# 64-row and 64-column attention matmuls made 128x128 in a two-layer streaming encoder step

## The chip, the cores and the metric

One core of a Trainium2 chip runs the whole step. The metric is the device time of one execution in microseconds (us). The engines are called TensorE (PE in the profile, its weight loads PEld), VectorE (DVE), ScalarE (ACT), GpSimd (POOL) and SyncE (SP, which only issues the transfers here). TensorE multiplies a stationary operand (`lhsT`, up to 128 rows by 128 columns) with a moving one (`rhs`, up to 512 columns) and writes PSUM; each matmul is preceded by a weight load.

## The reference, cut to what matters

Two layers run over 592 tokens: 16 meta tokens, 512 new prompt tokens and 64 new sample tokens, which have 256 cached keys of their own. Each layer normalises its input, projects it with one wide weight, and sums three gated branches (attention, a gated linear recurrence, causal pooling). The attention branch is what the change touches:

```python
s_idx = relu(einsum('bthd,bsd->bths', qi, ki))        # indexer: 4 heads of 64, one key of 64
score = einsum('bth,bths->bts', wi, s_idx)            # chunk-causal mask, then top k of the keys
logits = einsum('bthd,btjhd->bthj', q, k_gathered) * 64 ** -0.5   # 8 heads of 64
p = softmax(where(valid, logits, -inf))
out = einsum('bthj,btjhd->bthd', p, v_gathered)
```

Prompt queries see the meta tokens and the prompt up to the end of their own 64-token chunk, and keep 128 keys; sample queries see their 256 cached and 64 new keys and keep 80. The output holds the final activations, the new keys and values, and the recurrent states.

## The kernel before, in words

All weights are split into two float32r parts, and a projection is three matmuls per 128 input channels, all at line 266 (`mm3`). `c_project` makes 128 output channels for 296 (layer 0) or mostly 288 (layer 1) tokens at a time: 24 matmuls into one PSUM tile `acc` of three. `t_project` makes 256 or 324 channels for up to 128 tokens.

Attention and recurrence are written as Python generators, `index(j)`, `attend(j)`, `lru(g)`; after each projection `spend` credits them with a share of its time and runs steps of them, so that their instructions are emitted in between. The tile framework then orders every engine's instructions by simulating the program with its own costs: an instruction that is ready early in that simulation can be moved far ahead on its engine. Each engine executes its list in order. Buffers are slots of pools, and an instruction waits for its slot: `sc`, `rel` and `pt` have one, `lpa` (the logits) has two, the PSUM tiles `pq` and `pT` two each, and `pv` (the attention output) one.

Queries and keys lie with two heads of 64 along the partitions: `QK[:, 0:4]` queries, `QK[:, 4:8]` keys, `QI[:, 0:2]` indexer queries, `QI[:, 2]` the indexer key in both halves. Values `V` lie with keys along the partitions. Query tiles 0 to 3 are the prompt in blocks of 128, tile 4 is the sample. Prompt tile j has 144, 272, 400 or 528 keys (j+1 blocks of 128 and 16 more; 528 is done as two spans of 264).

- `index(j)`: for each of the four heads a 64-row matmul (line 434; for the sample 64x64 ones, written twice for both halves of the output, lines 429 and 431), a relu on ScalarE, a weighted sum on VectorE into `sc`; then 16 (sample: 10) rounds of max and replace on VectorE, and a bias tile.
- `attend(j)`, `logits`: for a pair of heads a 64-row matmul for each head and span (line 504; sample 64x64, lines 497 and 500), a masked minimum on VectorE (line 508), exp on ScalarE (514), reciprocal on VectorE (516), scaling on GpSimd (517, and 519 for the last 16 keys into `prem`).
- `values(u)`: for one head the blocks of probabilities are transposed on TensorE (529), copied to `pt` by ScalarE or VectorE (533, 531), and multiplied with 64 columns of values into one 64-partition half of `pv` (540). `rest(a)` adds the last 16 keys of four heads together with two 128x128 matmuls (547 to 551).
- At the end of `attend` one ScalarE copy puts `pv` into `QK` (568), where the queries were.

Other float32 matmuls on the full array are those of the recurrence gates (line 638, `lru`) and of the pooling map (741). Rotary (`rope`, lines 354 to 357) takes VectorE, GpSimd twice and VectorE again for each 128 channels. Attention on the projections' order: sample and first two tiles are indexed during the key and query projections; `attend(4)`, `attend(0)`, `index(2)`, `attend(1)`, `index(3)`, `attend(2)`, `attend(3)` follow during the gates, the first two branches and the pooling, and everything left is emitted at `side.drain()` ahead of the attention's own gate.

Of the kernel before, what the change touches and what calls it, by code (L numbers as in the profile page):

```python
# [9 lines left out]
F32 = mybir.dt.float32  # L10
F32R = mybir.dt.float32r
BF16 = mybir.dt.bfloat16
AF = mybir.ActivationFunctionType
# [3 lines left out]
D = 1024  # L17
NM = 16
SEQ = 512
NP = NM + SEQ  # L20
NS = 64
NT = NP + NS
# [18 lines left out]
class Side:  # L41
    """Steps of work emitted in between the projections."""
# [25 lines left out]
def build(ctx, tc, ap):  # L68
# [30 lines left out]
    nc.gpsimd.memset(vrem, 0.0)  # L99
    hb = const.tile([128, L, 8], F32)  # L100
# [167 lines left out]
    def t_project(ch, cols, src, evac, tiles=TILES):  # L268
        """Token-major: evac(t, psum) for each tile of tokens."""
# [16 lines left out]
    def c_project(ch, nk, src, pieces, evac, w=None, off=0, stride=128):  # L286
        """Channel-major: evac(piece, c0, n, psum) for each piece of the tokens."""
# [19 lines left out]
    def layer(l, xn, x_src, last):  # L307
# [7 lines left out]
        QK = big.tile([128, 8, NT], F32, name="QK", tag="big")  # L315
        VI = big.tile([128, 5 * 512 + 3 * NT], F32, name="VI", tag="big")
        V = VI[:, :2560].rearrange("p (t c) -> p t c", t=5)
        QI = VI[:, 2560:].rearrange("p (t c) -> p t c", t=3)
# [4 lines left out]
        vs = CH[0:64, 2304:2816]  # L323
# [72 lines left out]
        def ev_v(half_i):  # L396
            def f(t, c0, rows, p):
# [3 lines left out]
                if t == 4:  # L401
                    nc.sync.dma_start(vs[:, a], V[16:80, 4, a])
            return f

# [10 lines left out]
        def index(j):  # L415
# [5 lines left out]
            spans = [(0, 320)] if sample else kspan(j)  # L421
            for h in range(4):
                o = 64 * (h % 2)
                q = QI[o:o + 64, h // 2, q0:q0 + (64 if sample else 128)]
                for a, n in spans:
                    p = psq.tile([128, 512], F32, name="pq", tag="qk")
                    if sample:
                        for z in (0, 64):
                            nc.tensor.matmul(p[z:z + 64, 0:256], lhsT=q, rhs=kx[o:o + 64, :], start=True, stop=True)
                        for z in (0, 64):  # L430
                            nc.tensor.matmul(p[z:z + 64, 256:320], lhsT=q, rhs=QI[o:o + 64, 2, NP:NT],
                                             start=True, stop=True)
                    else:
                        nc.tensor.matmul(p[:rows, :n], lhsT=q, rhs=QI[o:o + 64, 2, a:a + n], start=True, stop=True)  # L434
# [26 lines left out]
        def attend(j):  # L461
            """The sample's tile (4) has two heads of 64 queries along the partitions; the others one of 128."""
# [7 lines left out]
            blocks = [(0, 128), (1, 128), (2, 64)] if sample else [(i, 128) for i in range(j + 1)]  # L470
            pv = psv.tile([128, 4, 128], F32, name="pv", tag="pv")
            P = {}
            if not sample:
# [465 lines left out]
```

## Time and profile before

| | us |
|---|---|
| three runs | 1294.51, 1295.75, 1297.30 (median 1295.75) |
| span of the profiled execution, first to last instruction | 1294.3 |
| PE busy in the span | 1266.2 (98%) |
| DVE busy | 745.7 (58%) |
| ACT busy | 467.4 (36%) |
| POOL busy | 284.2 (22%) |

The page gives the profiled execution by its span alone; the median of the runs lies 1.45 us above that span. A matmul's busy time in the profile is its modelled way through the array, about 0.3 us, while the next one starts after 0.13 us; so the time that a matmul costs is read from the starts of its neighbours, not from its own duration. A float32 matmul is two MATMUL rows (two passes), a float32r matmul or a transpose is one. The forms are written rows*columns of the stationary operand, then the moving operand.

### The profile page before, as it was taken

The numbers are of one execution on the slowest core, as the hardware profiler recorded it, in microseconds if no ns is written. First come the engines' busy times: TensorE is split into PE (matmuls) and PEld (weight loads), VectorE is DVE, ScalarE is ACT, GpSimd is POOL, SyncE is SP. The second block draws the span as 40 slices with busy tenths as digits, with TensorE's granted clock in tenths as the row PEclk, the third lists the DMA queues.
The fourth block names the chain that finished last, engine by engine and source line by source line (L and its number), as shares of the span: only waits on it lengthen the run. The fifth ranks groups of instructions, "written<-read, shape, count | busy, mean of one in ns | idle before, by whom it ended". The sixth has DMA issues, their size and how long they took to land.

```text
span 1294.3 us, 22304 instructions
## 1 busy us (share of the span) xinstructions
PE 1266.2 (98%) x9060; PEld 1177.7 (91%) x9060; DVE 745.7 (58%) x1588; ACT 467.4 (36%) x921; POOL 284.2 (22%) x329
## 2 busy tenths in 40 slices
PE   5999989999999999999999999899999999999998
PEld 5999978898988899999999999789799888999997
DVE  6388993665954334434363889848396543344343
ACT  5344543332333322332343446432333332233232
POOL 5122432021123320011012234311111332101121
PEclk9999999999999999999999999999999999999999
DMA  9321221221222022221353212112122212222212
GB/s 288 112 71 65 104 83 50 65 66 57 67 93 66 33 90 82 82 82 67 105 165 127 66 65 104 59 56 75 50 74 90 76 33 75 81 86 78 94 55 74
DMA packets 38024, 107.16 MB, mean 83 GB/s; under 512 B 6912, under 2 KB 10048, under 8 KB 37664
## 3 DMA queue, kind: packets, MB, share of 16 engines
q1 hardware_dynamic: 37920, 105.72, 25.0%
q8 instruction: 71, 1.16, 0.4%
q14 instruction: 33, 0.27, 0.1%
HBM read 95.35 MB, written 10.09 MB: 81 GB/s over the span
## 4 chain that ended last, share of the span: by engine, by line
PE 87%; DVE 9%; POOL 1%; issue 1%; ACT 1%; DMA 1%; SPq 0%; POOLq 0%; DVEq 0%; ACTq 0%
PE acc L266 73%; PE pv L540 4%; PE pq L504 3%; PE pT L529 2%; DVE wl L190 2%; PE pq L434 1%; DVE rt L354 1%; DVE lxc L628 1%; DVE sc L451 1%; PE pv L551 1%; PE pg L741 1%; DVE lT L654 1%; DVE m L450 1%; DVE QK L357 1%; POOL QK L356 1%
## 5 line engine op out<-in xcount | busy, mean ns | idle before, releaser
L266 PE MATMUL acc<-xh,wh 128*128 128x296 f32 (+1 forms) x1728 | 524.0, 303 | 0.0
L266 PE MATMUL acc<-xh,wl 128*128 128x296 f32 (+1 forms) x1728 | 521.5, 302 | 0.0
L266 PE MATMUL acc<-xl,wh 128*128 128x296 f32 (+1 forms) x1728 | 520.4, 301 | 0.0
L266 PEld LDWEIGHTS acc<-xh,wh 128*128 128x128 f32 x1728 | 326.7, 189 | 12.2 <-issue 8.0
L266 PEld LDWEIGHTS acc<-xl,wh 128*128 128x128 f32 x1728 | 327.2, 189 | 7.8 <-issue 5.3
L190 DVE TENSOR_TENSOR wl<-wr,wh 128x1024 fp32r<-128x1024 f32 (+1 forms) x158 | 210.7, 1335 | 212.1 <-ACT wh L189 209.2
L266 PEld LDWEIGHTS acc<-xh,wl 128*128 128x128 f32 x1728 | 325.5, 188 | 7.9 <-issue 5.6
L189 ACT ACTIVATE wh<-wr 128x1024 fp32r<-128x1024 f32 (+1 forms) x158 | 166.2, 1054 | 277.3 <-PE acc L266 256.8
L517 POOL TENSOR_SCALAR lpa<-lpa,mn 128x128 f32<-128x128 f32 (+4 forms) x72 | 84.2, 1170 | 281.2 <-DVE mn L516 238.7
L266 PE MATMUL acc<-yh,wh 128*128 128x296 f32 (+1 forms) x384 | 115.9, 302 | 0.0
L266 PE MATMUL acc<-yl,wh 128*128 128x296 f32 (+1 forms) x384 | 115.3, 300 | 0.0
L266 PE MATMUL acc<-yh,wl 128*128 128x296 f32 (+1 forms) x384 | 114.6, 299 | 0.0
L266 PE MATMUL acc<-wh,ml 128*128 128x256 f32 (+2 forms) x320 | 89.4, 281 | 0.0
L266 PE MATMUL acc<-wh,mh 128*128 128x256 f32 (+2 forms) x320 | 88.5, 280 | 0.0
L266 PE MATMUL acc<-wl,mh 128*128 128x256 f32 (+2 forms) x320 | 88.5, 280 | 0.0
L450 DVE MAX8 m<-sc 64x8 f32<-64x144 f32 (+4 forms) x148 | 74.7, 504 | 4.0 <-POOL sc L445 1.0
L266 PEld LDWEIGHTS acc<-yh,wh 128*128 128x128 f32 x384 | 72.3, 188 | 5.1 <-issue 4.2
L266 PEld LDWEIGHTS acc<-yl,wh 128*128 128x128 f32 x384 | 72.3, 188 | 2.9 <-issue 2.9
L266 PEld LDWEIGHTS acc<-yh,wl 128*128 128x128 f32 x384 | 72.2, 188 | 1.4 <-issue 1.4
L451 DVE MATCH_REPLACE8 sc<-m,sc 64x144 f32<-64x144 f32 (+4 forms) x148 | 72.5, 490 | 0.1
L514 ACT ACTIVATE lpa<-lpa,mn 128x144 f32<-128x144 f32 (+4 forms) x72 | 41.2, 572 | 72.6 <-DVE mn L508 70.1
L699 ACT ACTIVATE e<-acc 128x296 f32<-128x296 f32 (+1 forms) x96 | 38.9, 405 | 71.4 <-PE acc L266 71.3
(194 smaller groups left out, 1688.2 us busy)
## 6 DMA issues: line engine op xcount, KB each, us to landing
wr<-wc SPq DMA_DIRECT2D x108, 512.0 KB, 3.3
wr<-wb SPq DMA_DIRECT2D x24, 512.0 KB, 3.3
wr<-wo SPq DMA_DIRECT2D x16, 512.0 KB, 3.7
kT<-QK SPq DMA_DIRECT2D x2, 1184.0 KB, 4.2
xi<-xin SPq DMA_DIRECT2D x8, 256.0 KB, 7.6
wr<-wv SPq DMA_DIRECT2D x4, 512.0 KB, 6.4
v_p<-VI SPq DMA_DIRECT2D x16, 128.0 KB, 1.9
xo<-xin SPq DMA_DIRECT2D x8, 256.0 KB, 2.6
```

Source lines behind the costliest of these rows:

```text
L189: nc.scalar.activation(h[:, :size], r[:, :size], AF.Copy)
L190: nc.vector.tensor_sub(lo[:, :size], r[:, :size], h[:, :size].bitcast(F32))
L266: nc.tensor.matmul(out, lhsT=a, rhs=b, start=(i == 0), stop=(i == n - 1))
L354: nc.vector.stream_shuffle(t[:r, c0:], x[:, c0:], SWAP)
L450: nc.vector.max(m8[rr], sc[rr, :w])
L451: nc.vector.match_replace(sc[rr, :w], m8[rr], sc[rr, :w], TAKEN)
L504: nc.tensor.matmul(p[:, :n], lhsT=QK[o:o + 64, u // 2, q0:q0 + 128], rhs=QK[o:o + 64, 4 + u // 2, a:a + n], start=True, stop=True)
L514: nc.scalar.activation(t[:, :w], t[:, :w], AF.Exp, bias=mn[:, i:i + 1], scale=-1.0, accum_out=mn[:, 2:3])
L517: nc.gpsimd.tensor_scalar(t[:, :wm], t[:, :wm], mn[:, 3:4], None, op0=ALU.mult)
L529: nc.tensor.transpose(ps[:n, i], t[:, 128 * i:128 * i + n], ident)
L540: nc.tensor.matmul(pv[o:o + 64, h // 2, :nq], lhsT=val(i, n, h), rhs=pt[:n, i, c:c + nq], start=(i == 0 and (sample or u < 2)), stop=(samp ...
L699: nc.scalar.activation(e[:, c0:c0 + nn], p, AF.Tanh, scale=0.5)
```

## The change

Every attention and indexer matmul gets a stationary operand of 128 rows and 128 columns.

Logits and indexer scores: the queries of one head are copied by GpSimd into a tile whose other 64 rows stay zero, and the matmul runs over both heads' keys. For the indexer that tile is `qiz` (four heads; two copies for a prompt tile, four for the sample, made before the first head). For the prompt logits it is `qz`, two buffers of two heads each, kept behind `QK` and `VI` in their slots; two copies for each pair of heads. For the sample `qzs` has head 2u in rows and columns 0 to 63 and head 2u+1 in the others; two copies in all. The zeros are written in `late_loads`, once for each layer.

Values: `values` takes both heads of a pair, transposes both, copies both to a `pt` of twice the size, and multiplies 128 columns of values with 256 columns of probabilities. Half of the product is not wanted, and only the wanted halves are copied out. `pv` is now a tile for each four heads (`[128, 2, 2, 128]`, still one slot), copied out by two ScalarE instructions in `rest(a)`; `rest` has four matmuls instead of two. The sample's third block of keys is padded with zero rows in `vs` and zero probabilities.

To make room, `bd` (recurrence weights) and `gB` (norm weights) share one slot, which they take in turn: norm 0, recurrence 0, norm 1, recurrence 1, final norm.

```diff
+    qiz = const.tile([128, 4, 128], F32)
+    nc.gpsimd.memset(qiz, 0.0)
...
-        g = lay.tile([128, D], F32, name="gB")
+        g = lay.tile([128, D], F32, name="gB", tag="gb")
...
+        QK_ = big.tile([128, 8 * NT + 256], F32, name="QK", tag="big")
+        VI = big.tile([128, VE + 768], F32, name="VI", tag="big")
+        qz = [QK_[:, 8 * NT:].rearrange("p (t c) -> p t c", t=2),
+              VI[:, VE:VE + 256].rearrange("p (t c) -> p t c", t=2)]
+        qzs = VI[:, VE + 256:].rearrange("p (t c) -> p t c", t=4)
-        vs = CH[0:64, 2304:2816]
+        vs = CH[:, 2304:2816]
-        bd = lay.tile([128, 2, 4, 128], F32, name="bd")
+        bd = lay.tile([128, 2, 4, 128], F32, name="bd", tag="gb")
...
+            nc.gpsimd.memset(qz[0], 0.0)
+            nc.gpsimd.memset(VI[:, VE:], 0.0)
+            nc.gpsimd.memset(vs[64:128], 0.0)
...
+            for par in range(2):
+                o = 64 * par
+                for z in range(0, 128, nq):
+                    nc.gpsimd.tensor_copy(qiz[o:o + 64, par::2, z:z + nq], QI[o:o + 64, 0:2, q0:q0 + nq])
             for h in range(4):
-                o = 64 * (h % 2)
-                q = QI[o:o + 64, h // 2, q0:q0 + (64 if sample else 128)]
+                q = qiz[:, h]
...
-                        for z in (0, 64):
-                            nc.tensor.matmul(p[z:z + 64, 0:256], lhsT=q, rhs=kx[o:o + 64, :], start=True, stop=True)
...
+                        nc.tensor.matmul(p[:, 0:256], lhsT=q, rhs=kx, start=True, stop=True)
+                        nc.tensor.matmul(p[:, 256:320], lhsT=q, rhs=QI[:, 2, NP:NT], start=True, stop=True)
-                        nc.tensor.matmul(p[:rows, :n], lhsT=q, rhs=QI[o:o + 64, 2, a:a + n], start=True, stop=True)
+                        nc.tensor.matmul(p[:, :n], lhsT=q, rhs=QI[:, 2, a:a + n], start=True, stop=True)
...
+            if sample:
+                for o in (0, 64):
+                    nc.gpsimd.tensor_copy(qzs[o:o + 64, :, o:o + 64], QK[o:o + 64, 0:4, NP:NT])
...
+                if not sample:
+                    i = units[0] // 2
+                    for o in (0, 64):
+                        nc.gpsimd.tensor_copy(qz[i % 2][o:o + 64, o // 64], QK[o:o + 64, i, q0:q0 + 128])
...
-                            nc.tensor.matmul(p[:, :n], lhsT=QK[o:o + 64, u // 2, q0:q0 + 128],
-                                             rhs=QK[o:o + 64, 4 + u // 2, a:a + n], start=True, stop=True)
+                            nc.tensor.matmul(p[:, :n], lhsT=qz[u // 2 % 2][:, u % 2], rhs=QK[:, 4 + u // 2, a:a + n],
+                                             start=True, stop=True)
...
+            def values(units):
+                i = units[0] if sample else units[0] // 2
+                pt = tmp.tile([128, 4, 2, 128], F32, name="pt", tag="pt")
+                for n, u in enumerate(units):
+                    t = P.pop(u)
+                    ps = psm.tile([128, 4, 128], F32, name="pT", tag="ms")
+                    for k in range(nb):
+                        nc.tensor.transpose(ps[:, k], t[:, 128 * k:128 * k + 128], ident)
+                    if u % 2:
+                        nc.vector.tensor_copy(pt[:, :nb, n], ps[:, :nb])
+                    else:
+                        nc.scalar.activation(pt[:, :nb, n], ps[:, :nb], AF.Copy)
...
+                if i % 2 == 0:
+                    pvs[i // 2] = psv.tile([128, 2, 2, 128], F32, name="pv", tag="pv")
+                for k in range(nb):
+                    nc.tensor.matmul(pvs[i // 2][:, i % 2], lhsT=val(k, i), rhs=pt[:, k],
+                                     start=(k == 0 and i % 2 == 0), stop=False, skip_group_check=True)
...
-                for i in (2 * a, 2 * a + 1):
-                    nc.tensor.matmul(pv[:, i], lhsT=vrem[:, i], rhs=pr, start=False, stop=True,
-                                     skip_group_check=True)
+                for i in range(2):
+                    for n in range(2):
+                        nc.tensor.matmul(pv[:, i, n], lhsT=vrem[:, 2 * a + i], rhs=pr, start=False, stop=True,
+                                         skip_group_check=True)
+                for n in range(2):
+                    o = 64 * n
+                    nc.scalar.activation(QK[o:o + 64, 2 * a:2 * a + 2, q0:q0 + 128], pv[o:o + 64, :, n], AF.Copy)
...
-            nc.scalar.activation(QK[:, 0:4, q0:q0 + nq], pv[:, :, :nq], AF.Copy)
```

## Rows read from the trace of the kernel before

**Rows 1.** Page, part 4: shares of the chain that ended last.
```profile
PE 87%; DVE 9%; POOL 1%; issue 1%; ACT 1%; DMA 1%; SPq 0%; POOLq 0%; DVEq 0%; ACTq 0%
```

**Rows 2.** TensorE's waits: us in total, times, longest.
```profile
PE pq L581 <- DVE QK L357: 4.1, 2, 3.6
PE pq L497 <- DVE mn L508: 2.7, 1, 2.7
```

**Rows 3.** Busy us by stretch: PE, PEld, DVE, ACT, POOL, then clock, DMA, GB/s.
```profile
110.00:190.00 80.00, 75.45 (x526) 70.09 (x524) 76.06 (x175) 42.92 (x68) 29.66 (x28) 0.98 0.27 89
324.00:360.00 36.00, 36.00 (x260) 35.53 (x259) 34.31 (x70) 11.31 (x21) 5.49 (x10) 1.00 0.23 74
```

**Rows 4.** Line 266 alone in the two attention stretches: length, busy us, matmuls.
```profile
190.00:478.00 288.00, 221.19 (x1456) 1.00 0.20 64
822.00:1098.00 276.00, 209.74 (x1418) 1.00 0.20 65
```

**Rows 5.** Chain of waits, projections of 296 and 288 tokens: start, us, what.
```profile
232.00 3.00 PE acc L266 x22
...
1059.33 3.20 PE acc L266 x24
```

**Rows 6.** TensorE timeline at 426 us: start, us, line, tiles, forms, count.
```profile
426.52 0.38 PE L266 MATMUL acc<-xl,wh 128*128 128x296 f32 x1
426.83 0.71 PE L504 MATMUL pq<-QK 64*128 64x264 f32 x2
427.47 0.40 PE L266 MATMUL acc<-xh,wl 128*128 128x296 f32 x1
427.81 1.09 PE L540 MATMUL pv<-pt,VI 128*64 128x128 f32 x8
428.82 0.40 PE L266 MATMUL acc<-xh,wh 128*128 128x296 f32 x1
429.07 0.30 PE L266 MATMUL acc<-xl,wh 128*128 128x296 f32 x1
```

**Rows 7.** TensorE timeline at 87 us, float32 on the full array.
```profile
87.10 0.30 PE L266 MATMUL acc<-xh,wl 128*128 128x296 f32 x1
87.23 1.17 PE L638 MATMUL pg<-lxc,bd 128*128 128x298 f32 x4
88.02 0.52 PE L266 MATMUL acc<-xh,wh 128*128 128x296 f32 x1
88.38 0.30 PE L266 MATMUL acc<-xl,wh 128*128 128x296 f32 x1
```

**Rows 8.** TensorE timeline at 366 us, two heads' logits in a row.
```profile
366.43 0.30 PE L266 MATMUL acc<-xh,wl 128*128 128x296 f32 x1
366.65 0.94 PE L504 MATMUL pq<-QK 64*128 64x400 f32 x4
367.53 0.40 PE L266 MATMUL acc<-xh,wh 128*128 128x296 f32 x1
367.77 0.30 PE L266 MATMUL acc<-xl,wh 128*128 128x296 f32 x1
```

**Rows 9.** GpSimd groups by form: a small copy, a scaling of 128 columns.
```profile
L517 POOL TENSOR_SCALAR lpa<-lpa,mn 128x128 f32<-128x128 f32 x16 | 11.0, 690 | 54.7 <-DVE mn L516 54.7
L382 POOL COPY wd<-wt 4x64 f32<-4x64 f32 x2 | 0.5, 228 | 0.0
```

**Rows 10.** Timelines of VectorE and GpSimd near 123 us.
```profile
122.78 2.00 POOL L356 TENSOR_TENSOR QK<-QK,rope_c 128x592 f32<-128x592 f32 x1
123.39 2.04 DVE L628 SCALAR_TENSOR_TENSOR lxc<-CH,prm,lxc 128x595 f32<-128x595 f32 x1
127.21 0.82 DVE L628 SCALAR_TENSOR_TENSOR lxc<-CH,prm,lxc 128x595 f32<-128x595 f32 x1
```

**Rows 11.** Line 266 alone, from the start of attention to the denser VectorE stretches.
```profile
190.00:324.00 134.00, 103.08 (x688) 1.00 0.18 58
822.00:940.00 118.00, 86.98 (x576) 1.00 0.17 58
```

More of the change, by code (lines that the diff above doesn't have):

```diff
@@ L469, in attend @@
             b = bias.pop(j)
[L470 to L473, printed above, removed]
+            nb = 3 if sample else j + 1
+            if sample:
+                for o in (0, 64):
+                    nc.gpsimd.tensor_copy(qzs[o:o + 64, :, o:o + 64], QK[o:o + 64, 0:4, NP:NT])
+            else:
                 for h in range(NH):
@@ L494, in logits @@
                         if sample:
-                            q = [QK[z:z + 64, u, NP:NT] for z in (0, 64)]
-                            for z in (0, 64):
-                                nc.tensor.matmul(p[z:z + 64, 0:256], lhsT=q[z // 64], rhs=kc[z:z + 64, u, :],
-                                                 start=True, stop=True)
-                            for z in (0, 64):
-                                nc.tensor.matmul(p[z:z + 64, 256:320], lhsT=q[z // 64],
-                                                 rhs=QK[z:z + 64, 4 + u, NP:NT], start=True, stop=True)
-                        else:
-                            o = 64 * (u % 2)
-                            nc.tensor.matmul(p[:, :n], lhsT=QK[o:o + 64, u // 2, q0:q0 + 128],
-                                             rhs=QK[o:o + 64, 4 + u // 2, a:a + n], start=True, stop=True)
+                            nc.tensor.matmul(p[:, 0:256], lhsT=qzs[:, u], rhs=kc[:, u, :], start=True, stop=True)
+                            nc.tensor.matmul(p[:, 256:320], lhsT=qzs[:, u], rhs=QK[:, 4 + u, NP:NT],
+                                             start=True, stop=True)
+                        else:
+                            nc.tensor.matmul(p[:, :n], lhsT=qz[u // 2 % 2][:, u % 2], rhs=QK[:, 4 + u // 2, a:a + n],
+                                             start=True, stop=True)
                     for u in units:
@@ L517, in logits @@
                     nc.gpsimd.tensor_scalar(t[:, :wm], t[:, :wm], mn[:, 3:4], None, op0=ALU.mult)
-                    if not sample:
+                    if sample:
+                        nc.gpsimd.memset(t[:, w:384], 0.0)
+                    else:
                         nc.gpsimd.tensor_scalar(prem[:, u // 4, u % 4, 0:16], t[:, wm:w], mn[:, 3:4], None,
@@ L521, in logits @@
                     P[u] = t
-            def values(u):
-                t = P.pop(u)
-                pt = tmp.tile([128, 4, 128], F32, name="pt", tag="pt")
-                ps = psm.tile([128, 4, 128], F32, name="pT", tag="ms")
-                nf = sum(1 for _, n in blocks if n == 128)
-                for i, n in blocks:
-                    nc.tensor.transpose(ps[:n, i], t[:, 128 * i:128 * i + n], ident)
-                if u % 2:
-                    nc.vector.tensor_copy(pt[:, :nf], ps[:, :nf])
-                else:
-                    nc.scalar.activation(pt[:, :nf], ps[:, :nf], AF.Copy)
-                if sample:
-                    nc.scalar.activation(pt[:64, 2], ps[:64, 2], AF.Copy)
-                for h in ((2 * u, 2 * u + 1) if sample else (u,)):
-                    o = 64 * (h % 2)
-                    c = o if sample else 0
-                    for i, n in blocks:
-                        nc.tensor.matmul(pv[o:o + 64, h // 2, :nq], lhsT=val(i, n, h), rhs=pt[:n, i, c:c + nq],
-                                         start=(i == 0 and (sample or u < 2)), stop=(sample and i == 2),
-                                         skip_group_check=not sample)
+            def values(units):
[8 more added lines that the diff above has]
+                        nc.vector.tensor_copy(pt[:, :nb, n], ps[:, :nb])
+                    else:
+                        nc.scalar.activation(pt[:, :nb, n], ps[:, :nb], AF.Copy)
+                if sample:
+                    if i == 0:
+                        pvs[0] = psv.tile([128, 4, 128], F32, name="pv", tag="pv")
+                    for k in range(nb):
+                        nc.tensor.matmul(pvs[0][:, i], lhsT=val(k, i), rhs=pt[:, k, 0], start=(k == 0),
+                                         stop=(k == nb - 1))
+                    return
+                if i % 2 == 0:
+                    pvs[i // 2] = psv.tile([128, 2, 2, 128], F32, name="pv", tag="pv")
+                for k in range(nb):
+                    nc.tensor.matmul(pvs[i // 2][:, i % 2], lhsT=val(k, i), rhs=pt[:, k],
+                                     start=(k == 0 and i % 2 == 0), stop=False, skip_group_check=True)
@@ L557, in attend @@
                     yield w * 2.5
-                    values(u)
+                    values([u])
+                for o in (0, 64):
+                    nc.scalar.activation(QK[o:o + 64, 0:4, NP:NT], pvs[0][o:o + 64, :, o:o + 64], AF.Copy)
             else:
@@ L562, in attend @@
                     yield w * 2.5
-                    values(2 * u)
-                    values(2 * u + 1)
+                    values([2 * u, 2 * u + 1])
                     if u % 2:
```

21 lines of the change are left out of this document (11 added, 10 removed).

## The prediction

> **What bounds the kernel now.** I read first the chain of waits: TensorE holds 87% of it and VectorE 9% [rows 1], so a microsecond taken from TensorE's list is a microsecond of the kernel wherever VectorE does not hold it up. TensorE's own waits then show where that is: apart from the start, the two long ones are 3.6 us for the last rotary of layer 0 and 2.7 us for the minimum of the sample's logits in layer 1 [rows 2]. Both end the stretch in which tiles 4, 0 and 1 are indexed beside the recurrence and the rotaries: there VectorE is busy 76.06 of 80 us [rows 3]. In the attention stretches behind it the projections alone make 1456 and 1418 matmuls [rows 4]. They follow each other every 3.00/22 = 0.136 us in layer 0 and 3.20/24 = 0.133 us in layer 1 [rows 5]. So 288.0 - 1456 x 0.1364 = 89.5 us and 276.0 - 1418 x 0.1333 = 86.9 us of these stretches are spent on other matmuls. That is where the change works.
>
> **Why small forms cost more than their columns.** The timeline at 87 us has float32 matmuls on the full array: from 87.10 to 88.38 us are two projections (0.27) and four passes of 298 columns, so a pass costs (1.28 - 0.27)/4 = 0.252 us, or 0.846 ns a column, with nothing at either end [rows 7]. At 426 us the array changes its form twice: from 426.52 to 429.07 us are three projections (0.41), two passes of 264 columns on 64 rows and eight passes of 128 columns to 64 columns [rows 6]. At 0.846 ns a column these passes are 0.45 + 0.87 = 1.31 us, and they take 2.14: two visits to a small form cost 0.83 us on top. About half of it is seen ahead of and behind each visit, where the next start is 0.31 to 0.34 us away instead of 0.136.
>
> The opposite effect is there too. Two heads of 64 rows, 400 columns each, issued in a row at 366 us, take 367.77 - 366.43 - 0.27 = 1.07 us for four passes [rows 8], where four on the full array would take 4 x 400 x 0.846 = 1.35: the heads run partly together, and padding loses that. It is in the measured stretches already. The Trainium skill ("TensorE: Matmul & The Clock Gate", Part 3: Packing small matmuls) makes this the rule and speaks against the change: matmuls in different row groups run concurrently, and a small one takes as long as a full one. By that rule, with every two heads together, the logits and scores of these stretches would lose some 2 us a layer by padding, only the values would gain, some 10 us a layer, and the time would be near 1286. The trace agrees for such pairs as the one shown and not for the spans of 264, each of which stands alone [rows 6]; the totals above hold what was really shared, so the rule gets no chance of its own.
>
> **The change part by part, TensorE.** After it, each pass on the full array costs 0.846 ns a column. In one layer's stretch: prompt logits, 8 heads x (144 + 272 + 400 + 528) columns x 2 passes = 21,504 columns, 18.2 us. Scores of tiles 2 and 3, 4 x (400 + 528) x 2 = 7,424, 6.3 us. Prompt values, 4 pairs x 10 blocks x 256 x 2 = 20,480, 17.3 us (the same columns as before in half the matmuls). Sample values, 4 x 3 x 128 x 2 = 3,072, 2.6 us. The last keys, 4 tiles x 8 matmuls x 128 x 2 = 8,192, 6.9 us, twice what they were. Transposes, 100 x 128 columns in one pass, 10.8 us, unchanged. Sum 62.1 us; one unit of sample logits also lies in layer 0's stretch (+0.7) and six transposes lie ahead of layer 1's (-0.6). Before: the 16 pooling passes of each stretch (0.252 each, 4.0 us) and about 1 us for the meta tokens in layer 0 go off, which leaves 84.5 and 82.9 us. The saving is 84.5 - 62.8 + 82.9 - 61.5 = 43.1 us.
>
> Ahead of these stretches, in the indexing of tiles 4, 0 and 1 and the sample's logits, TensorE saves some 2.5 us a layer by the same prices (six or so lone score visits of 0.4 us each). I count that at nothing: TensorE ends that stretch waiting for VectorE [rows 2, 3], so it waits longer. The other end is -5 us.
>
> **GpSimd and VectorE.** Per layer 12 copies for `qiz`, 34 for `qz` and `qzs`, and seven zero fills. A copy of 64x128 isn't in the trace; a 4x64 copy takes 0.228 us and a scaling of 128 columns 0.690 [rows 9]. I take 0.45, so some 21 us a layer. GpSimd has the room: it is busy 29.66 of 80 us in the indexing stretch and 5.49 of 36 in a later one [rows 3]. But two things reach VectorE. First, a VectorE instruction beside a GpSimd one can grow: the same form took 2.04 us with a GpSimd multiply running and 0.82 alone [rows 10]. Eight copies a layer fall into the VectorE-bound stretch; between nothing and 8 x 0.69 = 5.5 us, I take 1.5. Second, the sample's first score now needs both rotated query chunks and four copies: one projection more, 48 x 0.136 = 6.5 us, and 1.8 us of copies. VectorE has other work then; between nothing and 6.5 us a layer, I take 1. Both layers: +5 us.
>
> **New waits on TensorE.** A prompt pair's logits wait for two copies behind whatever GpSimd's list holds, the scalings of the pair before above all; behind the waiting matmul stand all projections. The copies need only the rotated queries, so they can be placed early. In the attention stretches the trace has almost no TensorE wait, though every step there waits for another engine, so I take +2 us in all; the bounds are 0 and 40 groups of logits x 0.45 = 18 us. `pv` for the second four heads waits for two ScalarE copies that lie a pair's work earlier: hidden, or if not, under 1 us for each tile. Both `pt` halves are now filled side by side ahead of the values instead of one after the other with values between them: no cost. ScalarE gets three more short copies for each prompt tile and loses two kinds of others: nothing, it is nowhere near busy [rows 3]. The shared slot of `bd` and `gB`: the fill of `bd` for layer 1 moves behind the norm that ends layer 0, and its two loads with it on SP; the first gate matmul of layer 0 comes at 87 us [rows 7], deep in the layer, so I cost this at nothing; uncovered it is one load, 5 us or so by my estimate from the place of that matmul.
>
> **Sum.** 1294.3 (span) - 43.1 + 5 + 2 = 1258.2, and with the 1.45 us by which the median of the runs exceeds the span, 1259.7 us.
>
> **Rivals.**
> 1. VectorE takes part of it back. At 324 to 360 us it is busy 34.31 of 36 us [rows 3], and layer 1 has such a stretch from 940. If TensorE can't run ahead through these, what it saved before them is lost. The other matmuls before them are 134 - 688 x 0.1364 = 40.2 and 118 - 576 x 0.1333 = 41.2 us [rows 5, 11] of 89.5 and 86.9, so 46% of 43 us, 20 us: 1280. For it: two dense stretches. Against it: VectorE's work there comes out of the same order and moves forward too. Chance 0.18.
> 2. All of it and more: the saving ahead of the attention counts too and nothing is added, 1295.75 - 43 - 5 = 1248. Against it: the long waits [rows 2]. Chance 0.12.
> 3. Slower: GpSimd's list makes TensorE wait. If the copies stand behind the scalings of the pair before, each of the 32 prompt pairs makes TensorE wait for a scaling chain; with 3 us each that is 96 us, and 1295.75 - 43 + 5 + 96 = 1354. It decides from 43/32 = 1.3 us a pair. For it: GpSimd runs in order. Against it: the copies are ready long before, and the order of each list comes from a simulation that sees that. Chance 0.05.
> 4. The change doesn't do what it says: the extra cost belongs to float32 next to the projections, not to the form. Then nothing is saved, the last keys cost 7 us more and VectorE's 5 stay: 1308. Against it: the gate matmuls [rows 7], where float32 on the full array costs its columns alone. Chance 0.02.
>
> The forecast itself has 0.63, with its own range 1250 to 1270. The range for 8 times in 10 reaches to rivals 1 and 2: 1246 to 1281. A change within 0.2%, 2.6 us, can't be told from none. Faster: 0.63 + 0.18 + 0.12 less some 0.01 for a rival 1 far beyond its price = 0.92; slower: 0.07 from rivals 3 and 4, of which 0.01 goes to no change, with the other 0.01: same 0.02, slower 0.06.
>
> **What the profile after would show.** Line for line: logits and values as 128*128 with half as many passes of values; next starts of 0.13 us ahead of and behind them, no 0.31 to 0.34; the attention stretches shorter by about 21 us each, with the projections' spacing as it was; TensorE's wait for the last rotary as long as before or longer. Against me: TensorE waiting for GpSimd copies at the logits, gaps in the projections behind VectorE, a pass on the full array that costs clearly more than 0.85 ns a column, or an indexing stretch longer by over 5 us.

## The result, and the profile after

The changed kernel takes 1256.86 us (median, 1253.99 to 1258.17) against 1296.53 us for the kernel before on the same chip: 0.9689 of its time, 95% interval 0.9673 to 0.9705. Predicted were 1259.7 us, with a range of 1246 to 1281. The profiled execution has a span of 1256.4 us, 37.9 less than before.

The page of the changed kernel, parts 1 and 4 (busy time by engine; shares of the chain that ended last). `L266` of before is `L268` here, the logits are `L518`, the indexer scores `L446`, the values `L562`, the last keys `L574`.

```profile
PE 1222.0 (97%) x8852; PEld 1193.1 (95%) x8852; DVE 747.3 (59%) x1588; ACT 472.6 (38%) x939; POOL 328.6 (26%) x436
PE 86%; DVE 10%; issue 1%; POOL 1%; DMA 1%; ACT 1%; SPq 0%; POOLq 0%; DVEq 0%; ACTq 0%
```

The chain is still TensorE's, with nearly the shares of [rows 1]. TensorE's busy time went down by 44.2 us, the span by less: something was given back. GpSimd is busy 44.4 us longer, mostly with the copies and fills, and holds no more of the chain than before. The timeline of TensorE in the changed kernel near 410 us, to be laid beside [rows 6]:

```profile
409.23 0.30 PE L268 MATMUL acc<-xh,wl 128*128 128x296 f32 x1
409.37 0.61 PE L518 MATMUL pq<-QK,VI 128*128 128x264 f32 x2
409.62 0.49 PE L268 MATMUL acc<-xh,wh 128*128 128x296 f32 x1
409.95 0.30 PE L268 MATMUL acc<-xl,wh 128*128 128x296 f32 x1
410.08 1.89 PE L562 MATMUL pv<-pt,VI 128*128 128x256 f32 x8
411.81 0.61 PE L518 MATMUL pq<-QK,VI 128*128 128x264 f32 x2
```

From 409.23 to 409.95 are two projections (0.27) and the two passes of 264 columns: 0.45 us, where the same logits on 64 rows take 0.84 (shown below, with the first experiment). The eight value passes of 256 columns take 411.81 - 410.08 = 1.73 us, 0.845 ns a column, and serve two heads; before, eight passes served one. No next start of 0.31 to 0.34 us is left here: the start of `L518` comes 0.14 us after the projection ahead of it, and that of `L562` 0.13.

To see where the time went, the start of the k-th projection matmul is compared between two traces; both kernels have the same projections in the same number. Gain on the kernel before, in us, by stretch of that list (to the 1000th: start and indexing of layer 0; to the 2600th: attention of layer 0; to the 4600th: feed-forward of layer 0 and start of layer 1; to the 4800th: most of layer 1's indexing; then its attention; nothing changes after it). In the last stretch the sample's logits and the waits beside them stand ahead of layer 1's attention. The rows below the first are experiments, told further on:

```
kernel                         0-1000  -2600  -4600  -4800   -end    sum
changed kernel                  -2.6   +21.9   +0.5   -3.6  +21.7  +37.9
the same, another execution     -1.7   +21.0   +0.6   -3.7  +21.8  +38.0
values alone                    -1.7    +9.1   -0.1    0.0   +7.9  +15.2
scores and logits alone         +0.6   +12.2   +0.7   -3.7  +11.9  +21.7
pairs, 64-column values         -0.6   +15.2   +0.6   -4.7  +16.1  +26.6
no copies                       +0.6   +21.3   +0.9   -0.5  +21.1  +43.4
copies made, not read           -2.5   +21.8   +0.9   -0.6  +22.0  +41.6
last keys once                  -0.2   +25.6   +0.5   -3.6  +25.3  +47.6
last keys once, ScalarE copies  -0.3   +25.7   +0.5   -3.3  +23.6  +46.2
```

So the two attention stretches gained 43.6 us and the rest lost 5.7. The first column has to be read with care: the twelve profiled executions of the changed kernel and its variants are 0.6 to 3.7 us late at the 200th projection, some 50 us in, though their code differs there only in a few zero fills and the place of one set-up, and TensorE's first wait alone, for the first normalised tokens, lasts from 7.7 to 10.1 us. TensorE's waits in the changed kernel (total us, times, longest), against [rows 2]:

```profile
PE pq L446 <- DVE sc L449: 6.4, 2, 3.3
PE pq L607 <- DVE QK L368: 3.2, 2, 1.8
PE pq L514 <- POOL VI L485: 1.6, 1, 1.6
```

The wait of 2.7 us for the sample's minimum is gone, one of 1.6 for a query copy and one of 1.5 for VectorE's `e` (line 701) stand in its place, and the indexer scores now wait 3.3 and 3.1 us where the longest such wait was 0.5. They wait for VectorE to read the scores ahead of them out of PSUM. In layer 0 part of that comes off the waits for the rotary, which were 4.1 us; in layer 1 nothing else gets shorter in that stretch.

The busy time by stretch in the changed kernel (PE, PEld, DVE, ACT, POOL, clock, DMA, GB/s), against [rows 3]:

```profile
110.00:190.00 80.00, 73.65 (x510) 70.96 (x510) 75.39 (x169) 42.00 (x68) 36.06 (x36) 0.98 0.25 85
324.00:360.00 36.00, 36.00 (x256) 35.29 (x255) 29.09 (x56) 11.33 (x21) 3.56 (x8) 1.00 0.24 81
300.00:336.00 36.00, 36.00 (x254) 35.05 (x254) 32.75 (x68) 10.90 (x22) 7.88 (x13) 1.00 0.24 81
```

The indexing stretch is as full of VectorE's work as before. The dense stretch at 324 to 360 is not: that work moved forward with TensorE, to 300 to 336, and TensorE is busy all through it.

### The profile page after: what moved, and what is told of

It is laid out like the page before. It is cut to its first block, busy times and chain, and to the rows that moved or that the text cites. A ratio compares the mean times of both kernels' runs of the same rounds, so it can differ in the third digit from the quotient of the medians.

```text
span 1256.4 us, 22038 instructions
## 1 busy us (share of the span) xinstructions
PE 1222.0 (97%) x8852; PEld 1193.1 (95%) x8852; DVE 747.3 (59%) x1588; ACT 472.6 (38%) x939; POOL 328.6 (26%) x436
## 4 chain that ended last, share of the span: by engine, by line
PE 86%; DVE 10%; issue 1%; POOL 1%; DMA 1%; ACT 1%; SPq 0%; POOLq 0%; DVEq 0%; ACTq 0%
PE acc L268 73%; PE pq L518 3%; PE pv L562 3%; DVE wl L192 2%; PE pT L547 2%; DVE lxc L654 1%; PE pv L574 1%; PE pq L446 1%; DVE sc L463 1%; DVE m L462 1%; DVE rt L365 1%; DVE QK L368 1%; PE pg L767 1%; DVE CH L682 1%; DMA gB<-gall 1%
## 5 line engine op out<-in xcount | busy, mean ns | idle before, releaser
L268 PE MATMUL acc<-xh,wh 128*128 128x296 f32 (+1 forms) x1728 | 529.7, 307 | 1.5 <-DVE e L701 1.5
L268 PE MATMUL acc<-xh,wl 128*128 128x296 f32 (+1 forms) x1728 | 523.3, 303 | 0.0
L268 PE MATMUL acc<-xl,wh 128*128 128x296 f32 (+1 forms) x1728 | 521.0, 302 | 0.0
L268 PEld LDWEIGHTS acc<-xh,wh 128*128 128x128 f32 x1728 | 327.7, 190 | 5.2 <-DVE e L701 1.7
L268 PEld LDWEIGHTS acc<-xl,wh 128*128 128x128 f32 x1728 | 327.9, 190 | 3.1
L268 PEld LDWEIGHTS acc<-xh,wl 128*128 128x128 f32 x1728 | 326.3, 189 | 1.9
L268 PE MATMUL acc<-yh,wh 128*128 128x296 f32 (+1 forms) x384 | 117.5, 306 | 0.0
L268 PE MATMUL acc<-yl,wh 128*128 128x296 f32 (+1 forms) x384 | 116.3, 303 | 0.0
L268 PE MATMUL acc<-yh,wl 128*128 128x296 f32 (+1 forms) x384 | 116.0, 302 | 0.0
L531 POOL TENSOR_SCALAR lpa<-lpa,mn 128x128 f32<-128x128 f32 (+4 forms) x72 | 81.3, 1129 | 99.8 <-DVE mn L530 83.3
L268 PE MATMUL acc<-wh,ml 128*128 128x256 f32 (+2 forms) x320 | 89.5, 281 | 0.0
L268 PE MATMUL acc<-wh,mh 128*128 128x256 f32 (+2 forms) x320 | 88.6, 280 | 0.0
L268 PE MATMUL acc<-wl,mh 128*128 128x256 f32 (+2 forms) x320 | 88.5, 281 | 0.0
L268 PEld LDWEIGHTS acc<-yh,wh 128*128 128x128 f32 x384 | 72.3, 188 | 1.6
L268 PEld LDWEIGHTS acc<-yl,wh 128*128 128x128 f32 x384 | 72.3, 188 | 1.3
L268 PEld LDWEIGHTS acc<-yh,wl 128*128 128x128 f32 x384 | 72.3, 188 | 1.1
L740 POOL TENSOR_TENSOR e<-m,e 128x592 f32<-128x592 f32 (+1 forms) x16 | 23.2, 1448 | 184.4 <-DVE e L734 184.4
```

Source lines behind the costliest of these rows:

```text
L268: nc.tensor.matmul(out, lhsT=a, rhs=b, start=(i == 0), stop=(i == n - 1))
L531: nc.gpsimd.tensor_scalar(t[:, :wm], t[:, :wm], mn[:, 3:4], None, op0=ALU.mult)
L740: nc.gpsimd.tensor_tensor(e[:, C0:], m[:, j, C0:], e[:, C0:], op=ALU.add)
```

## The experiments

The theory: every visit of the array to a small form costs a fixed price beyond its columns, and that is what the change saves. The rivals: the saving comes from fewer matmuls, or from another order of the work. "Before" beside each run is the kernel before on the same chip.

**Values alone, and scores and logits alone.** The first keeps the new values and puts back 64-row logits and scores; the second does the opposite.

```diff
 values alone
-                q = qiz[:, h]
+                q = QI[o:o + 64, h // 2, q0:q0 + (64 if sample else 128)]
 scores and logits alone
-                    nc.tensor.matmul(pvs[i // 2][:, i % 2], lhsT=val(k, i), rhs=pt[:, k], ...
+                        nc.tensor.matmul(pv[o:o + 64, h // 2, :nq], lhsT=val1(i, n, h), rhs=pt[:n, i, c:c + nq], ...
```

> Only the values take the new form; logits and scores stay on 64 rows, without their copies. Theory (the form of the array costs, visit by visit): against the changed kernel the visits of logits and scores come back, about 27 us, and some 3 us go with the copies, so 1281 us. Rival 1 (the shorter chain of the paired values pays): near 1257. Rival 2 (half as many value matmuls and weight loads pay): near 1257.

> Only logits and scores are padded; the values are as in the kernel before, one head after the other on 64 columns, and the last keys are two matmuls. Theory: against the changed kernel 64 visits to the 64-column form at 0.34 us come back (22 us) and the sample's 6 us, and the doubled last keys (7 us) go: 1278 us. Rivals 1 and 2: the padding alone saves nothing, near 1296.

Measured: 1280.89 us for values alone (0.9876 [0.9861, 0.9891] of before, 1297.09) and 1275.88 for scores and logits alone (0.984 [0.9823, 0.9856]). The timeline of the first shows the old price where the old form stayed:

```profile
418.15 0.29 PE L266 MATMUL acc<-xh,wl 128*128 128x296 f32 x1
418.38 0.71 PE L512 MATMUL pq<-QK 64*128 64x264 f32 x2
419.01 0.41 PE L266 MATMUL acc<-xh,wh 128*128 128x296 f32 x1
419.26 0.30 PE L266 MATMUL acc<-xl,wh 128*128 128x296 f32 x1
```

419.26 - 418.15 - 0.27 = 0.84 us for the two passes of 264, 0.39 above their columns. The price is nearly the same at every visit. In the kernel before, 22 lone visits of two passes of 264 columns took 0.83 to 0.85 us, those of 144 columns 0.63, those of 400 1.06 (medians): 0.39 above the columns each time. Visits of 4, 6 and 8 passes of 128 columns to 64 columns took 0.78, 0.99 and 1.21: 0.34 or 0.35 above, whatever the number of matmuls.

TensorE's weight loads, first in this kernel and then (last line) in the changed one:

```profile
418.38 0.29 PEld L512 LDWEIGHTS pq<-QK 64*128 64x128 f32 x2 [0.17 <-issue]
419.01 0.19 PEld L266 LDWEIGHTS acc<-xh,wh 128*128 128x128 f32 x1 [0.34 <-issue]
409.23 0.33 PEld L518 LDWEIGHTS pq<-QK,VI 128*128 128x128 f32 x2
```

On the full array the load of `L518` starts at 409.23, with the projection ahead of it and 0.13 us before its own matmul at 409.37. At the change to 64 rows, and at the change back, load and matmul start together (418.38 and 419.01), and nothing of the load runs beside the matmul ahead. In the kernel before, a load leads its matmul by 0.132 us in the median of those that keep the full array, and by 0.002 us in the median of the 472 changes of form. So the price lies at the two changes, on the way in and on the way out. Why the load doesn't run ahead there, no run shows.

Logits and scores keep their number of prompt matmuls in the second kernel and still give 21.2 us. So the number of matmuls is not what counts. The two gains add up to 37.4 us; the whole change gives 39.7 against its own runs of before (40.7 in the repeated run below).

**Pairs as in the change, values of 64 columns.** Both heads are transposed and copied first, as in the change, but multiplied with 64 columns of values each.

```diff
+                for n in range(2):
+                    o = 64 * n
+                    for k in range(nb):
+                        nc.tensor.matmul(pv[o:o + 64, i, :nq], lhsT=val(k, i)[:, o:o + 64], rhs=rhs, ...
```

> As the changed kernel, pairs of heads with both halves of the probabilities copied before the values, but each value matmul again on 64 columns of one head, and the last keys two matmuls. Theory: one visit for a pair instead of two, so 32 x 0.34 = 11 us and the sample's 6 us come back and 7 us of the last keys go: 1267 us, 11 us under the padding-only kernel. Rival 1 (the paired chain pays, not the form): near 1257 or, with the last keys, 1250. Rival 2 (the number of matmuls pays): as the padding-only kernel, near 1278.

Measured: 1269.72 us (0.979 [0.9775, 0.9804]). It is faster than scores and logits alone with the same number of matmul rows (8996 in both profiles), and far from 1257, so neither the number of matmuls nor the paired order is what pays. The size was wrong: 6.2 us under that kernel, not 11. The two heads' products were expected to share one visit, but the written order is not the order on the engine: its list has 69 stretches of 128*64 where scores and logits alone had 87 (and 16 of 64*64 beside such). By an estimate at 0.34 us a visit, 18 fewer are 6.1 us. A lone one still pays, in its timeline:

```profile
443.63 0.29 PE L268 MATMUL acc<-xl,wh 128*128 128x296 f32 x1
443.85 1.09 PE L557 MATMUL pv<-pt,VI 128*64 128x128 f32 x8
444.87 0.41 PE L268 MATMUL acc<-xh,wl 128*128 128x296 f32 x1
445.12 0.29 PE L268 MATMUL acc<-xh,wh 128*128 128x296 f32 x1
```

445.12 - 443.63 - 0.27 = 1.22 us against 0.87 by columns: 0.35 a visit. Against the version further down with the same value and last-key columns (last keys once), the attention stretches of this one are 50.9 - 31.3 = 19.6 us longer for 69 visits, 0.28 each on average.

**No copies.**

```diff
-                    nc.gpsimd.tensor_copy(qiz[o:o + 64, par::2, z:z + nq], QI[o:o + 64, 0:2, q0:q0 + nq])
-                    nc.gpsimd.tensor_copy(qzs[o:o + 64, :, o:o + 64], QK[o:o + 64, 0:4, NP:NT])
-                        nc.gpsimd.tensor_copy(qz[i % 2][o:o + 64, o // 64], QK[o:o + 64, i, q0:q0 + 128])
```

> The changed kernel without GpSimd's copies of the queries, so that the padded queries are all zero; everything else runs as it did. If the copies cost what I put down for them (VectorE slowed beside them, the first scores of the sample waiting, TensorE waiting for them), 2 to 7 us less than the changed kernel, 1250 to 1255. If they are hidden: 1257 within 2 us.

Measured: 1253.92 us (0.9669 [0.9654, 0.9685]), 2.9 less than the changed kernel; the intervals overlap (0.9673 to 0.9705 there), so the stretches decide. By the table the attention stretches don't gain without the copies; the indexing does. So the 32 prompt copies a layer are hidden, and what is given back lies in the indexing. Of the 3.2 us of the first column, though, 1.3 are there at the 200th projection, long before the first copy (78 us). Layer 1 has no such doubt: from the 4600th projection to the end the changed kernel gains 18.1 us on before in both its profiles, this one 20.5.

**Copies on ScalarE; copies made but not read.** The first stands on the version with the last keys once, the second on the changed kernel.

```diff
 ScalarE copies
-                    nc.gpsimd.tensor_copy(qiz[o:o + 64, par::2, z:z + nq], QI[o:o + 64, 0:2, q0:q0 + nq])
+                    nc.scalar.activation(qiz[o:o + 64, par::2, z:z + nq], QI[o:o + 64, 0:2, q0:q0 + nq], AF.Copy)
 (the sample's qzs likewise)
 copies made, not read
-                q = qiz[:, h]
+                q = ident
-                            nc.tensor.matmul(p[:, 0:256], lhsT=qzs[:, u], rhs=kc[:, u, :], start=True, stop=True)
+                            nc.tensor.matmul(p[:, 0:256], lhsT=ident, rhs=kc[:, u, :], start=True, stop=True)
```

> The version with the last keys once (1250.0 us), but the copies of the indexer queries and of the sample's queries (12 + 2 a layer) are made by ScalarE instead of GpSimd; the copies for the prompt logits stay on GpSimd. Leaving all copies out gained 3 us, all of it in the indexing of both layers. If GpSimd is the reason (a copy waits behind its rotary multiplies, or slows VectorE beside it): about 3 us less, 1247, with less TensorE waiting at the scores in layer 1. If it is that the scores need a copy at all, behind both rotated chunks, or the other order of VectorE's list that comes with it: 1250, with the same wait of 3 us at the scores.

> The changed kernel (1256.86 us) with all its copies made, but the indexer scores and the sample's logits multiply by the identity instead of the copied queries, so no matmul there waits for a copy or for the rotated chunks behind it (these scores and logits are left out). Leaving out the copies of all queries gained 3 us. If that came from the wait for them (all four heads behind both rotated chunks and the copies): 1254, without TensorE's wait of 3 us at the scores in layer 1. If it came from the copies' own time on GpSimd, or from the order of the lists that they bring: 1257.

Measured: 1249.84 us for ScalarE (0.9623 [0.961, 0.9636]), no different from 1250.0; and 1252.67 for copies made but not read (0.9661 [0.9648, 0.9674]), as without copies; its interval still touches that of the changed kernel (0.9667 to 0.9694), so the stretches of the table and the waits decide. TensorE's waits from 745 to 795 us (layer 1's indexing) of the changed kernel, and of the one that doesn't read the copies:

```profile
PE pq L446 <- DVE sc L449: 3.3, 1, 3.3
```

```profile
PE pq L446 <- DVE sc L449: 1.6, 1, 1.6
PE pq L514 <- DVE mn L522: 1.6, 1, 1.6
```

GpSimd makes all 24 `qiz` copies in that kernel too. So neither their time on GpSimd nor VectorE being slowed beside them is the cause: moving them to ScalarE gained nothing (0.3 us in layer 1's indexing, less than was lost behind it), and taking away only the dependence of the scores and the sample's logits on them gave the 3 us of layer 1 back. VectorE's list ahead of the read that ends the wait (`L449`), in the changed kernel and then in the one that doesn't read the copies:

```profile
765.65 0.78 DVE L677 SCALAR_TENSOR_TENSOR lT<-lthr,lT 128x595 f32<-128x595 f32 x1
767.15 0.78 DVE L676 SCALAR_TENSOR_TENSOR lthi<-lthi,lxc 128x595 f32<-128x595 f32 x1
767.85 0.49 DVE L449 TENSOR_SCALAR sc<-pq,wq 128x272 f32<-128x272 f32 x1
```

```profile
762.42 0.39 DVE L466 TENSOR_SCALAR bias<-sc 64x144 bf16<-64x144 f32 x1
762.85 0.50 DVE L449 TENSOR_SCALAR sc<-pq,wq 128x272 f32<-128x272 f32 x1
```

VectorE is busy all through the wait. In the changed kernel two recurrence steps of 0.78 us stand inside it, ahead of the read; without the dependence, and without the copies, they don't, and the wait is 1.6 us shorter. The kernel with ScalarE copies has both steps there too, and a wait of 2.9 us. So by these lists it is the order of VectorE's work, which comes with the dependence, that makes the wait longer; no run changes that order alone. The rest of the 3 us is for the most part the slower clock behind the wait (last section), which neither kernel without the dependence has in layer 1.

**Last keys once.** The padded halves of the last 16 keys are computed once for two heads; VectorE adds them.

```diff
-                    for n in range(2):
-                        nc.tensor.matmul(pv[:, i, n], lhsT=vrem[:, 2 * a + i], rhs=pr, start=False, stop=True, ...
+                    nc.tensor.matmul(ps[:, 1 + i], lhsT=vrem[:, 2 * a + i], rhs=pr, start=True, stop=True)
+                nc.scalar.activation(QK[:, 2 * a:2 * a + 2, q0:q0 + 128], ps[:, 1:3], AF.Copy)
...
+                    nc.vector.tensor_tensor(d, pv[o:o + 64, :, n], d, op=ALU.add)
```

> The changed kernel (1256.86 us), but the last 16 keys of each head are multiplied once for both heads (16 products of 128 columns in two passes fewer, over both layers) and VectorE adds the halves. Theory (what counts is time on TensorE's list, at 0.846 ns a column): 16 products x 4 x 128 columns become 2 x 128 each, so 64 passes of 0.108 us fall away, 6.9 us less: 1250. Rival (VectorE, which gets 16 more additions of some 0.5 us in its dense stretches, holds TensorE back instead): 1257 or more.

> The changed kernel unaltered, beside the others on the same chip: 1256.9 by its own median, and the same stretches lost or won in the profile (2.5 us late at 36 us, 22 us gained in layer 0's attention, 3.6 us lost in layer 1's indexing). If one of these is an accident of one execution it is missing here.

Measured side by side: 1250.02 us (0.963 [0.9616, 0.9643]) and 1256.8 (0.9681 [0.9667, 0.9694]); the intervals don't touch. The 6.8 us are those of the 64 passes taken off (64 left of 128). The additions, by the view of that line in this kernel:

```profile
L578 DVE TENSOR_TENSOR QK<-pv,QK x32: 395/422/429, 223.8 to 1046.5; 64x256 f32<-64x256 f32 x32
```

32 additions of 0.42 us, 13.4 us of VectorE, cost nothing: in the attention stretches VectorE is not the bound. The repeated kernel shows the same stretches gained and lost; 22 us was 21.0 in layer 0 this time.

**Set-up later.**

```diff
         def late_loads():
-                setup_params()
...
         indexer_keys()
+        if l == 0:
+            setup_params()
```

> The changed kernel, but the small set-up of the recurrence parameters in layer 0 is emitted after the indexer keys instead of with the late loads, so that it can't stand ahead of the copy that the first projections need. If the 2.5 us by which the profile of the changed kernel is late at 36 us come from that set-up beside a GpSimd fill: 1254.5. If that set-up only shares the place and something else (the loads, the shared slot) delays the first projections: 1257, with TensorE's wait of 2.3 us at 26 us still there.

> Last keys once and set-up later together, as a version that might beat both kernels. If the two are independent, as the theory has it: 1256.86 - 7 - 2.5 = 1247.5. If VectorE takes back what TensorE saves: 1254.5 to 1257.

Measured: 1256.95 us (0.9677 [0.9664, 0.969]), and 1249.5 with the last keys once (0.9627 [0.9614, 0.964]). The edit didn't do what it says: VectorE's timeline shows the set-up at the same place, in this kernel and in the changed one:

```profile
23.73 1.72 DVE L111 SCALAR_TENSOR_TENSOR spt<-prm 128x8 f32<-128x8 f32 x1
```

```profile
23.51 1.72 DVE L111 SCALAR_TENSOR_TENSOR spt<-prm 128x8 f32<-128x8 f32 x1
```

The simulated order put it back, so the edit tested nothing. The repeated run of the changed kernel does: there that instruction took 0.15 us, and the 200th projection is 2.4 us late all the same, as against 2.5 here. So its growth is not what makes the start late; what does stays open. The delay isn't caught up either. The 400th projection, at 80 us, is only 0.6 us late, but because the sample's indexer scores stand behind it in the changed kernel and ahead of it in the kernel before; the 600th is 2.5 us late again.

**Tile 2's logits as pairs of 64 rows.** On the version with the last keys once.

```diff
+                            r = slice(o, o + 64) if j == 2 else slice(0, 128)
+                            q = QK[r, u // 2, q0:q0 + 128] if j == 2 else qz[u // 2 % 2][:, u % 2]
+                            nc.tensor.matmul(p[:, :n], lhsT=q, rhs=QK[r, 4 + u // 2, a:a + n], ...
```

> The version with the last keys once (1250.0 us), but the prompt logits of tile 2 (400 keys) go back to 64 rows, the two heads of a pair one after the other, without their copies. Prices from the traces of before and after: a pair run together costs 1.067 us on 64 rows and 1.341 padded, a lone head of 400 on 64 rows 1.06 against 0.67. Theory (a fixed price for each visit, and the two heads share the array): if all 8 pairs stand together, 8 x 0.27 = 2.2 us less, 1247.8; with the order of before, some 6 together and 4 heads alone, no difference, 1250. Rival (64 rows are always worse here, the pair's 1.067 was luck of its place): every head costs 0.39 more, 16 x 0.39 = 6 us, 1256.

Measured: 1248.71 us (0.9618 [0.9604, 0.9631]); not told apart from 1250.02. The prices are in the timelines: first a lone head and then a pair of heads in this kernel, then the same pair padded (version with the last keys once).

```profile
304.24 0.29 PE L268 MATMUL acc<-yh,wl 128*128 128x296 f32 x1
304.46 0.94 PE L521 MATMUL pq<-QK 64*128 64x400 f32 x2
305.33 0.41 PE L268 MATMUL acc<-yh,wh 128*128 128x296 f32 x1
305.58 0.30 PE L268 MATMUL acc<-yl,wh 128*128 128x296 f32 x1
...
913.77 0.29 PE L268 MATMUL acc<-yh,wl 128*128 128x288 f32 x1
914.00 0.94 PE L521 MATMUL pq<-QK 64*128 64x400 f32 x4
914.87 0.40 PE L268 MATMUL acc<-yh,wh 128*128 128x288 f32 x1
915.10 0.29 PE L268 MATMUL acc<-yl,wh 128*128 128x288 f32 x1
```

```profile
912.47 0.29 PE L268 MATMUL acc<-yh,wl 128*128 128x288 f32 x1
912.60 1.51 PE L518 MATMUL pq<-QK 128*128 128x400 f32 x4
913.63 0.60 PE L268 MATMUL acc<-yh,wh 128*128 128x288 f32 x1
914.07 0.30 PE L268 MATMUL acc<-yl,wh 128*128 128x288 f32 x1
```

Less two projections, the pair takes 1.07 us, the lone head also 1.07, the padded pair 1.34. Two heads in different rows of the array cost as much as one, as [rows 8] had it, and the rival by which the small form is always worse falls. Six pairs stand together in this kernel's list and four heads alone: 6 x 0.27 gained and 4 x 0.39 lost, which is nothing, as the expectation had it for that order. With 0.39 us a visit and 0.846 ns a column, a pair of two passes each wins over the full array where 2 x n x 0.846 ns exceeds 0.39 us, from some 230 columns, and a lone head never does; that limit is an estimate from these prices. The Trainium skill ("TensorE: Matmul & The Clock Gate", Part 3: Packing small matmuls) says that small matmuls in different rows of the array can run at the same time. The trace agrees where two of them are neighbours in the list, as in the pair shown.

## Why the prediction was right, and where it was not

- **Where the time is and what a visit costs: right.** The attention stretches were to give 21.7 and 21.4 us and gave 21.9 and 21.7. They are not quite the same stretches: the measured ones begin earlier and hold most of the sample's logits, whose saving the prediction had left out. From the 1040th projection on (190 us, where its stretch of layer 0 begins) 20.4 us are gained, in both executions. The prices on the full array came out as worked out from one row of the gate matmuls [rows 7]: 0.45 us for 2 x 264 columns, 1.73 for 8 x 256, 1.34 for 4 x 400 (1.35 foretold). That was possible because the stretch was taken as a total from the count of projections [rows 4, 5], and not as a sum of matmul durations, which overlap.
- **The rule that spoke against the change** had 1286 us; 1256.86 decides against it as a time. It fails on what the timelines said: the values and the spans of 264 stand alone.
- **Last keys twice what they were: right**, 6.9 us foretold, 6.8 given back when they are done once.
- **The indexing's own saving counted at nothing: right.** Without any copy the stretches before attention are 0.6 us ahead in layer 0 (1.8 from the 200th projection on), and layer 1's loses 0.5.
- **Copies and VectorE, +5: right in its size by luck, wrong in its cause.** The stretches outside attention lost 5.7 us. But 1.5 of 2.5 us a layer were to come from VectorE slowed beside GpSimd, and the copies on ScalarE gained nothing. The row that stood for "alone" [rows 10] had GpSimd copies beside it too (127.11 to 128.07 us), so it was no sign that copies slow VectorE. The other 1 us was put on the sample's first score; the new wait is at the scores of prompt tile 1 (272 columns), through the order of VectorE's list, and in layer 1 it costs about 3 us, three times that term. In layer 0 the loss is 1.7 to 2.6 us, and as much is already there at 49 us, before any copy; its cause is open.
- **New waits of TensorE, +2: too much.** In the attention stretches none is left for a `qz` copy; the one wait for a copy (1.6 us, sample) replaces a longer one. From the 4800th projection on TensorE waits 3.0 us in all, where it waited 3.5 before. The wait for the last rotary, forecast to be as long as before or longer, is 1.8 us instead of 3.6.
- **Copies at 0.45 us: right.** `L505` has means of 0.41 and 0.38 us, `L437` 0.49 and 0.54; the sample's four, of twice the width, 0.84.
- **Rival 1, VectorE's dense stretches take half back: wrong.** That work moved forward along with TensorE, as the argument against the rival said; even 13.4 us more of VectorE cost nothing there.
- **Rival 2, the saving ahead of attention counts too and nothing is added: wrong.** The stretches outside attention lost 5.7 us; even without the copies the time is 1253.92, not 1248.
- **Rival 3, GpSimd's list makes TensorE wait at every pair: wrong**, no pair waits. **Rival 4, the cost belongs to float32: wrong**, since form alone removed it.
- **The shared slot of `bd` and `gB`**: no wait for it shows in TensorE's list; it was not tried alone. Every variant has it too, so it may have a part in the late start. The 5 us for an uncovered load don't follow from the place of a matmul; the loads `wr` and `xi` of the kernel before land in 3.3 to 7.6 us (medians), and no run shows this one uncovered.

The sum hit because its large term was right. That it hit so closely is luck: its small errors (too little for the scores' wait and the start, too much for the copies' waits) nearly cancel.

## What to carry to other kernels

On an engine whose list is full, read the price of an operation from the starts of its neighbours, and ask whether it changes the array's form: here a lone small matmul paid 0.35 to 0.39 us for that, while padded with zeros it cost its columns alone. Two small ones side by side in different rows cost as much as one, but only if the engine's list really has them side by side. What such a change adds as preparation was free in the attention stretches, where the engine that makes the copies had slack. It cost time in the indexing, where TensorE waits for VectorE and the new dependence changed the order of VectorE's list: look there for what is given back. And compare two traces at places where both lists have done the same work.

## What the runs showed of the hardware

A wait can cost more than its length. After the 3.25 us that the scores wait in layer 1 of the changed kernel, TensorE's matmuls follow each other at 0.24 us instead of 0.133 for a while:

```profile
768.40 1.10 PE L446 MATMUL pq<-VI,qiz 128*128 128x272 f32 x2 [3.25 <-DVE sc L449]
...
769.53 0.45 PE L268 MATMUL acc<-xl,wh 128*128 128x288 f32 x1
769.77 0.45 PE L268 MATMUL acc<-xh,wl 128*128 128x288 f32 x1
...
772.25 0.29 PE L268 MATMUL acc<-xl,wh 128*128 128x288 f32 x1
```

The windows of the same stretch have the granted clock (the figure before the last two):

```profile
768.00:771.00 3.00, 2.60 (x10) 2.37 (x11) 3.00 (x7) 0.00 (x0) 0.16 (x1) 0.60 0.33 101
771.00:774.00 3.00, 3.00 (x21) 3.00 (x21) 3.00 (x3) 1.46 (x2) 3.00 (x2) 0.83 0.37 146
774.00:778.00 4.00, 4.00 (x33) 4.00 (x32) 4.00 (x6) 1.00 (x3) 1.99 (x4) 1.00 0.00 0
```

The engine stood idle, worked on at the lower of its two levels (1.2 GHz) and was back at 2.4 GHz by 774 us. From 769.53 to 772.25 us twelve projections take 2.72 us instead of 1.60: 1.1 us on top of the wait. Not every such wait does this. The 2.7 us for the sample's minimum in the kernel before left the clock at 1.00 (814 to 818 us). At the end of the scores' wait of 3.1 us in layer 0 the granted clock was 1.00 in one execution of the changed kernel and 0.50 in the other (148.3 to 151.7 us).

A small VectorE instruction can grow tenfold: the 128x8 instruction at 23.51 us took 1.72 us in the changed kernel, and 0.15 in the kernel before and in the repeated run of the changed one. Where it is long, it ends with a GpSimd multiply of 128x512 that began behind it: in the changed kernel the multiply runs from 23.95 to 25.21 us and the instruction ends at 25.23. In the kernel before it had ended (at 23.78) before that multiply began at 24.15. That the multiply is the cause was not tested.
